# Second block's latent attention: the scores of the next two query tiles written ahead of the weighted sums, and the rotary parts of all heads projected first

## The chip, the cores and the metric

The kernel is one program on one core of a Trainium2 chip. The engines are TensorE (PE, with its weight loads shown apart as PEld), VectorE (DVE), ScalarE (ACT), GpSimd (POOL) and SyncE (SP), whose queue issues every DMA of the part that is changed. Each engine runs its instructions in the order in which the program holds them. The metric is the device time of one execution in microseconds (us); smaller is better.

## The reference, cut to what matters

Two blocks of two layers each on 512 tokens of width 1024. The change is in the latent attention ("MLA") of the second block, which runs once in each of its two layers: 4 heads, each query and key made of 128 plain and 64 rotary columns, and the rotary part of the key shared by all heads.

```
def mla_branch(c_q, c_kv, k_rope, pos, q_norm, w_uq, kv_norm, w_ukv):
    q = (rmsnorm(c_q, q_norm) @ w_uq).reshape(B, S, MLA_HEADS, MLA_NOPE + MLA_ROPE)
    q_nope = q[..., :MLA_NOPE]
    q_rope = apply_rope_2(q[..., MLA_NOPE:], pos)
    kv = (rmsnorm(c_kv, kv_norm) @ w_ukv).reshape(B, S, MLA_HEADS, MLA_NOPE + MLA_V)
    k_nope, v = kv[..., :MLA_NOPE], kv[..., MLA_NOPE:]
    k_r = apply_rope_2(k_rope, pos)
...
        s = (jnp.einsum('bqhd,bkhd->bhqk', qn, k_nope)
             + jnp.einsum('bqhr,bkr->bhqk', qr, k_r))
        prob = jax.nn.softmax(s.astype(jnp.float32) * scale, axis=-1).astype(v.dtype)
        return jnp.einsum('bhqk,bkhd->bqhd', prob, v)
```

The result is multiplied by a gate, joined with a gated linear attention ("GLA"), projected by `w_out`, and then a second gate multiplies a projection of a further input `p` ("PLE").

## The kernel before, in words

Every value is held as a pair of a rounded part and its rest, so that a product is three matmuls (high times high, high times low, low times high). `split` (L298 to L300) makes such a pair: ACT casts to the high part (L299), DVE subtracts it to get the low part (L300). `wload` (L170 to L188) loads weights by DMA into one of three raw buffers (`wr`), casts them on ACT (L183) and subtracts on DVE (L186).

The program is written in one order and then put in another: a scheduler takes the instructions with the priorities that the code gives, estimates when each can start, and writes each engine's order. It may move an instruction ahead of others that stand before it in the code, so what the code writes is not what the engines run.

`layer2` runs one layer. Generators for the two halves of the GLA, the output gates, the low-rank inputs, the key's rotation, the normalisation scales and the attention are advanced one step at a time by the string `steps2` (L93): `0` and `1` are GLA halves, `g` gates, `c` low-rank inputs, `r` `key_rope`, `l` `scales`, `m` and `v` steps of `mla`.

`rope2` (L1223) rotates a tile: it needs the tile with its 32-row groups swapped, which DMAs from SBUF to SBUF make (L1235 to L1238), then DVE multiplies by cosine and sine (L1241, L1242), adds (L1243), and splits. `scales` sums squares into one PSUM bank (`pv`), and `lowrank_scale` (L1207 to L1221) turns them into factors by small matmuls, five short DVE instructions (L1214 to L1220) and a power on POOL (L211). The factors of the keys are spread over a tile, `rkb` (L1117), by which every key is multiplied when it leaves PSUM (L1548).

In `mla`, `proj_head(h)` projects keys and queries of head h; for heads 0 and 2 it also projects and rotates the rotary parts of two heads. A head's 512 queries are taken as two units of two 128-row query tiles. For a unit the code writes the scores of each tile (six matmuls into a bank of tag `ps`) with its `softmax` (L495 and L497 on DVE, the exponential L499 on ACT, L501 on DVE, the scaling L502 on ACT), then the transposes of the four key blocks (L1614, into the banks `pt`, `ga`, `gb` in turn), their split, and the weighted sum (twelve matmuls into `pv`), which DVE multiplies into the gate (L1626). At a head's end the gated result is split (`C<-L`). The PLE projections (L1063) are written in the last head.

PSUM has eight banks: two for `pp` (all projections), two for `ps`, one each for `pt`, `pv`, `ga` and `gb`. A tile's bank is free for the next tile of its tag when its last reader is done. SBUF tiles of 512 columns come from rings: `M` (25 buffers), `C` (20), `L` (13).

Of the kernel before, what the change touches and what calls it, by code (L numbers as in the profile page):

```python
# [11 lines left out]
F32R = mybir.dt.float32r  # L12
# [3 lines left out]
ALU = mybir.AluOpType  # L16
# [4 lines left out]
P = 128  # L21
D = 1024
KT = 8
SEQ = 512
# [53 lines left out]
class Net:  # L78
# [11 lines left out]
             "kkkkqqccggthhccqqiiccppppppggthhccqqiikkkkccppppppggthhccqqiiccppppppggthhcciipppppp")  # L90


    steps2 = "00" + "g0g1g" + "01g0" + "0100" + "cccc" + "1rlm" + "g1g1g1g1" + "v1"  # L93
    bprio, sprio = 300, 500
    wshare_mla = 0

# [31 lines left out]
    def al(self, role, dt=F32):  # L128
        pool, tag, bufs, w = self.roles[role]
        return pool.tile([P, w], dt, tag=tag, bufs=bufs, name=self.nm(tag))  # L130
# [912 lines left out]
        return xs  # L1043


    def ple_proj(self, l):

        nc = self.nc
        xs = []
        for k in range(2):  # L1050
            x = self.C()
            nc.sync.dma_start(x, self.a["pT"][l, k])
            h = (self.C(F32R), self.C(F32R))
            self.split(h[0], h[1], x)
            xs.append(h)
        out = []
        for c in range(2):
            w = self.wload(self.a["w_ple_proj"][l, c], 2, 512)
            for i in range(4):
                ps = self.ps("pp")  # L1060
                self.proj(ps, w, i * P, (i + 1) * P, xs, [(0, SEQ)])
                y = self.C()
                nc.scalar.activation(y, ps, AF.Copy, scale=0.5)  # L1063
                out.append(y)
        return out

    def trig(self):

# [151 lines left out]
        nc.vector.tensor_tensor(z, y, r, ALU.mult)  # L1220
        return z  # L1221

    def rope2(self, src, n, al, tmp):  # L1223


        nc = self.nc
        if n == P:
            x = tmp()
            nc.scalar.copy(x, src)
            rot, own = x, src  # L1230
        else:
            rot, own = src, tmp()
            for b in range(0, P, n):
                nc.sync.dma_start(own[b:b + n, :], src[0:n, :])
        sw = tmp()  # L1235
        for b in range(0, P, 32):
            o = (b ^ 32) % n
            nc.sync.dma_start(sw[b:b + 32, :], rot[o:o + 32, :])  # L1238
        y = tmp()
        for i, c in enumerate((slice(0, 256), slice(256, 512))):  # L1240
            nc.vector.tensor_tensor(y[:, c], own[:, c], self.cos[i], ALU.mult)  # L1241
            nc.vector.tensor_tensor(sw[:, c], sw[:, c], self.sin[i], ALU.mult)  # L1242
        nc.vector.tensor_tensor(y, y, sw, ALU.add)  # L1243
        a, b = al(F32R), al(F32R)
        self.split(a, b, y)
        return a, b

    def layer2(self, l, h, st):
        nc, tc, a = self.nc, self.tc, self.a
        S4 = [(0, SEQ)]  # L1250
# [65 lines left out]
        kr = []  # L1316

        def key_rope():
            kr.append(self.rope2(sm, 64, self.M, self.C))
            yield  # L1320

        ms, sc = [None] * KT, {}
# [11 lines left out]
        pts = []  # L1334
# [191 lines left out]
    def mla(self, l, cq, ckv, kr, sc, sgd, md, ms, pts):  # L1526


        nc, a = self.nc, self.a
        S4 = [(0, SEQ)]  # L1530
        rkb, rkv, qsc = sc["kvb"], sc["kv"], sc["q"]
        krh, krl = kr[0]
        qr, qk = {}, {}
        wk = {}

        def proj_head(h):
            if h % 2 == 0:
                w = self.wload(a["w_uq"][l, 2], 3, 256)
                ps = self.ps("pp")
                self.proj(ps, w, (h // 2) * P, (h // 2 + 1) * P, cq, S4)  # L1540
                qr[h // 2] = self.rope2(ps, P, self.M, self.M)
                wk["q"] = self.wload(a["w_uq"][l, h // 2], 3, 256)
                wk["k"] = self.wload(a["w_ukv"][l, 0][:, :, 256 * (h // 2):256 * (h // 2) + 256], 2, 256)
            m = slice((h % 2) * P, (h % 2 + 1) * P)
# [10 lines left out]
            qk[h] = (kh, kl, qh, ql)  # L1555

        proj_head(0)
        yield

        w = self.wload(a["w_ukv"][l, 1], 2, 512)  # L1560
        vs = []
        for t in range(4):
            ps = self.ps("pp")
            for k in range(2):
                xh, xl = ckv[k]
                c = slice(t * P, (t + 1) * P)
                self.mm(ps, xh[:, c], w.hi(k, 0, 512), k == 0, False)
                self.mm(ps, xh[:, c], w.lo(k, 0, 512), False, False)
                self.mm(ps, xl[:, c], w.hi(k, 0, 512), False, k == 1)
# [4 lines left out]
            vs.append((vh, vl))  # L1574
        yield
        for h in range(4):
            if h < 3:
                proj_head(h + 1)
            else:
                pts += self.ple_proj(l)  # L1580
            if h == 2:
                for hd in range(4, 8):
                    t = self.C()
                    nc.sync.dma_start(t, md[hd])
                    x, y = self.L(F32R), self.L(F32R)
                    self.split(x, y, t)
                    ms[hd] = (x, y)
            kh, kl, qh, ql = qk.pop(h)
            rh, rl = qr[h // 2]
            rr = slice(64 * (h % 2), 64 * (h % 2) + 64)  # L1590
            sg = self.L()
            nc.sync.dma_start(sg, sgd[h])
            for tp in range(2):
                pr = []
                for j in range(2):
                    t = 2 * tp + j
                    c = slice(t * P, (t + 1) * P)
                    ps = self.ps("ps")
                    self.mm(ps, qh[:, c], kh, True, False)
                    self.mm(ps, qh[:, c], kl, False, False)  # L1600
                    self.mm(ps, ql[:, c], kh, False, False)
                    self.mm(ps, rh[rr, c], krh[rr], False, False)
                    self.mm(ps, rh[rr, c], krl[rr], False, False)
                    self.mm(ps, rl[rr, c], krh[rr], False, True)
                    p = self.M()
                    self.softmax(ps, SEQ, qsc[:, t:t + 1], p)
                    pr.append(p)
                po = self.ps("pv")
                for kk in range(0, 4, 2):
                    self.npt += 1  # L1610
                    pt = self.ps(("pt", "ga", "gb")[self.npt % 3])
                    for i in range(2):
                        for j in range(2):
                            nc.tensor.transpose(pt[:, i * 256 + j * P:i * 256 + (j + 1) * P],  # L1614
                                                pr[j][:, (kk + i) * P:(kk + i + 1) * P], self.ident)
                    ph, pl = self.M(F32R), self.M(F32R)
                    self.split(ph, pl, pt)
                    for i in range(2):
                        kt = kk + i
                        vc = slice(h * P, (h + 1) * P)  # L1620
                        ss = slice(i * 256, (i + 1) * 256)
                        self.mm(po[:, :256], vs[kt][0][:, vc], ph[:, ss], kt == 0, False)
                        self.mm(po[:, :256], vs[kt][0][:, vc], pl[:, ss], False, False)
                        self.mm(po[:, :256], vs[kt][1][:, vc], ph[:, ss], False, kt == 3)
                sc = sg[:, tp * 256:(tp + 1) * 256]
                nc.vector.tensor_tensor(sc, po[:, :256], sc, ALU.mult)  # L1626
            al = self.C if h < 3 else self.L
            x, y = al(F32R), al(F32R)
            self.split(x, y, sg)
            ms[h] = (x, y)  # L1630
            yield


# [125 lines left out]
```

## Time and profile before

| what | value |
|---|---|
| median of 3 runs | 3402.8 us (3402.74 to 3403.55) |
| the profiled execution, its own time | 3398.06 us |
| span of the profiled execution | 3396.3 us |
| mean granted TensorE clock | 0.962 of full speed |
| TensorE matmul busy | 3189.1 us (94%) |
| VectorE busy | 2134.7 us (63%) |
| ScalarE busy | 1414.4 us (42%) |

The span is what the hardware profiler saw between the first and the last instruction; the execution's own time lies 1.8 us above it, and 4.7 us below the median of the runs. A busy share is an average over stages with different limits. The granted clock is 1.0 at 2.4 GHz and 0.5 at 1.2 GHz, TensorE's two levels; a number between them is a mean over a stretch.

### The profile page before, as it was taken

How to read it: one execution, taken by the hardware profiler on the slowest of the kernel's cores; microseconds unless marked ns; L12 is line 12 of the kernel's file. 1: busy time of each engine (PE TensorE's matmuls, PEld its weight loads, DVE VectorE, ACT ScalarE, POOL GpSimd, SP SyncE). 2: the span in 40 equal slices, each digit the busy share in tenths (PEclk: the TensorE clock that was granted, in tenths of full speed). 3: DMA queues.
4: the chain of work that ended last, by engine and by line, in shares of the span. 5: the costliest groups of instructions: out<-in, count | busy, mean ns of one | idle time of the engine just before them, and what ended most of it. 6: DMA issues, size and time to landing. Idle time of an engine off the chain costs nothing. (4 is left out here: it accounts for less than half of the span.)

```text
span 3396.3 us, 46629 instructions
## 1 busy us (share of the span) xinstructions
PE 3189.1 (94%) x18622; PEld 2663.2 (78%) x18622; DVE 2134.7 (63%) x3158; ACT 1414.4 (42%) x2406; POOL 413.2 (12%) x489
## 2 busy tenths in 40 slices
PE   7999999999999999998999989899998898998898
PEld 4887887878778888887888867888887666996677
DVE  6795968744554444446997966755556655666555
ACT  3444343444432122224444445532346435564464
POOL 2130322201000000002112311000001200122001
PEclk8999998999999999998999999999998998999999
DMA  6232312133333432232222233433243232442323
GB/s 254 70 125 84 122 58 69 60 118 101 100 118 132 141 119 63 60 109 88 72 70 91 78 121 113 150 98 99 88 126 110 88 99 70 156 155 80 99 91 119
DMA packets 112808, 353.45 MB, mean 104 GB/s; under 512 B 13328, under 2 KB 20048, under 8 KB 107472
## 3 DMA queue, kind: packets, MB, share of 16 engines
q1 hardware_dynamic: 112592, 350.48, 32.1%
q8 instruction: 146, 2.39, 0.3%
q14 instruction: 70, 0.57, 0.1%
HBM read 327.10 MB, written 21.23 MB: 103 GB/s over the span
## 5 line engine op out<-in xcount | busy, mean ns | idle before, releaser
L186 DVE TENSOR_TENSOR wl<-wr,wh 128x1024 fp32r<-128x1024 f32 (+1 forms) x482 | 582.7, 1211 | 354.8 <-ACT wh L183 350.2
L183 ACT CAST wh<-wr 128x1024 fp32r<-128x1024 f32 (+1 forms) x482 | 490.8, 1020 | 739.3 <-PE pp L191 692.7
L191 PE MATMUL pp<-A,wh 128*128 128x512 f32 (+1 forms) x3392 | 779.8, 345 | 14.5 <-DVE A L296 5.2
L191 PE MATMUL pp<-C,wh 128*128 128x512 f32 (+1 forms) x2328 | 650.6, 366 | 27.5 <-DVE M L1548 11.0
L191 PEld LDWEIGHTS pp<-A,wh 128*128 128x128 f32 x3392 | 537.1, 190 | 127.3 <-issue 19.7
L191 PEld LDWEIGHTS pp<-C,wh 128*128 128x128 f32 x2328 | 414.8, 192 | 111.3 <-DVE M L1548 12.7
L191 PE MATMUL pp<-A,wl 128*128 128x512 f32 (+1 forms) x1696 | 463.2, 342 | 0.0
L191 PE MATMUL pp<-C,wl 128*128 128x512 f32 (+1 forms) x1164 | 421.3, 363 | 0.0
L191 PE MATMUL pp<-B,wh 128*128 128x512 f32 (+1 forms) x1296 | 316.7, 351 | 0.1
L191 PE MATMUL pp<-M,wh 128*128 128x256 f32 (+1 forms) x1280 | 294.3, 325 | 14.5 <-ACT M L1132 7.1
L191 PEld LDWEIGHTS pp<-A,wl 128*128 128x128 f32 x1696 | 272.6, 190 | 41.5 <-issue 1.9
L599 DVE SCALAR_TENSOR_TENSOR W<-W,cw,W 128x783 f32<-128x783 f32 x240 | 275.5, 1152 | 2.6
L191 PEld LDWEIGHTS pp<-C,wl 128*128 128x128 f32 x1164 | 222.3, 191 | 36.6 <-issue 1.1
L191 PEld LDWEIGHTS pp<-M,wh 128*128 128x128 f32 x1280 | 217.2, 196 | 42.4 <-issue 10.4
L191 PEld LDWEIGHTS pp<-B,wh 128*128 128x128 f32 x1296 | 212.3, 188 | 38.4 <-issue 2.1
L211 POOL TENSOR_TENSOR s<-s,nhalf 128x2 f32<-128x2 f32 (+4 forms) x40 | 54.4, 1360 | 1433.7 <-DVE s L277 1416.4
L191 PE MATMUL pp<-M,wl 128*128 128x256 f32 (+1 forms) x640 | 204.8, 321 | 0.0
L599 DVE SCALAR_TENSOR_TENSOR W<-U,cw,W 128x512 f32<-128x512 f32 x240 | 192.8, 804 | 3.5
L191 PE MATMUL pp<-B,wl 128*128 128x512 f32 (+1 forms) x648 | 194.0, 351 | 0.0
L886 DVE SCALAR_TENSOR_TENSOR B<-pp,cols,B 128x511 f32<-128x511 f32 x66 | 43.4, 658 | 214.7 <-ACT B L883 214.7
L851 DVE SCALAR_TENSOR_TENSOR X<-pp,g,X 128x512 f32<-128x512 f32 (+1 forms) x128 | 77.0, 631 | 146.9 <-PE pp L191 146.6
L883 ACT ACTIVATE B<-pp,cols 128x768 f32<-128x768 f32 (+1 forms) x44 | 38.9, 885 | 231.0 <-PE pp L191 231.0
(402 smaller groups left out, 4753.8 us busy)
## 6 DMA issues: line engine op xcount, KB each, us to landing
wr<-w_in SPq DMA_DIRECT2D x184, 512.0 KB, 3.8
wr<-w_up SPq DMA_DIRECT2D x96, 512.0 KB, 3.8
wa<-w_ada SPq DMA_DIRECT2D x40, 1024.0 KB, 5.0
wr<-w_out SPq DMA_DIRECT2D x64, 512.0 KB, 3.9
wr<-w_down SPq DMA_DIRECT2D x48, 512.0 KB, 3.6
wr<-w_ple_gate SPq DMA_DIRECT2D x32, 512.0 KB, 3.9
Z<-w_ada SPq DMA_DIRECT2D x16, 512.0 KB, 8.4
wr<-conv_pw SPq DMA_DIRECT2D x16, 512.0 KB, 3.8
```

The lines of the kernel that those rows point to most:

```text
L183: nc.scalar.copy(hi[:, :n], raw[:, :n])
L186: eng.tensor_tensor(lo[:, :n], raw[:, :n], hi[:, :n].bitcast(F32), ALU.subtract)
L191: return self.nc.tensor.matmul(out, l, r, start=start, stop=stop)
L211: self.nc.gpsimd.tensor_tensor(y, x, self.nhalf[:, :n], ALU.pow)
L599: nc.vector.scalar_tensor_tensor(y, gl[:, i:i + no], ws[:, i:i + 1], y, ALU.mult, ALU.add)
L851: nc.vector.scalar_tensor_tensor(xs[t][:, c0:c0 + sn], ps[:, c0:c0 + sn], g5[:, t, q:q + 1], xs[t][:, c0:c0 + sn], ALU.mult, ALU.add)
L883: nc.scalar.activation(y[:, :n], pa[:, :n], AF.Identity, bias=self.col(l, "fdw_b")[:, f:f + 1], scale=cw[:, 1:2])
L886: nc.vector.scalar_tensor_tensor(y[:, c0 + 1:e], pa[:, c0:e - 1], cw[:, 0:1], y[:, c0 + 1:e], ALU.mult, ALU.add)
```

## The change

The code of one unit is cut in two functions, `scores(h, tp)` and `weighted(h, tp, pr, sg)`. The loop over the eight units of a layer writes the scores of the next unit before the weighted sum of the present one. `rope2` is cut into `rope_rows` (copy out of PSUM and the swapping DMAs) and `rope_turn` (the arithmetic, now in place and thus one tile less). `query_rows` projects the rotary parts of all four heads, from one load of their weights, before head 0; their `rope_turn` stands after the value projections. The key's rotation is a step ahead of `scales`, its arithmetic behind it (`1rlrm`). The PLE projections are written in two portions, one in each unit of the last head, and the loads of the four GLA results one at a time after units 3 to 6.

```
-    steps2 = "00" + "g0g1g" + "01g0" + "0100" + "cccc" + "1rlm" + "g1g1g1g1" + "v1"
+    steps2 = "00" + "g0g1g" + "01g0" + "0100" + "cccc" + "1rlrm" + "g1g1g1g1" + "v1"
...
-    def rope2(self, src, n, al, tmp):
+    def rope_rows(self, src, n, tmp):
+        nc = self.nc
+        own, sw = tmp(), tmp()
         if n == P:
-            x = tmp()
-            nc.scalar.copy(x, src)
-            rot, own = x, src
+            nc.scalar.copy(own, src)
+            rot = own
...
+        return own, sw
+
+    def rope_turn(self, own, sw, al):
...
+            nc.vector.tensor_tensor(own[:, c], own[:, c], self.cos[i], ALU.mult)
...
         def key_rope():
-            kr.append(self.rope2(sm, 64, self.M, self.C))
+            rows = self.rope_rows(sm, 64, self.C)
+            yield
+            kr.append(self.rope_turn(*rows, self.M))
             yield
...
+        def query_rows():
+            w = self.wload(a["w_uq"][l, 2], 3, 256)
+            rows = []
+            for i in range(2):
+                ps = self.ps("pp")
+                self.proj(ps, w, i * P, (i + 1) * P, cq, S4)
+                rows.append(self.rope_rows(ps, P, self.M))
+            return rows
         def proj_head(h):
             if h % 2 == 0:
-                w = self.wload(a["w_uq"][l, 2], 3, 256)
-                ps = self.ps("pp")
-                self.proj(ps, w, (h // 2) * P, (h // 2 + 1) * P, cq, S4)
-                qr[h // 2] = self.rope2(ps, P, self.M, self.M)
...
+        units = [(h, tp) for h in range(4) for tp in range(2)]
+        emb = self.ple_proj(l, pts)
+        pr = scores(*units[0])
+        for (h, tp), then in zip(units, units[1:] + [None]):
+            if tp == 0:
+                sg = self.L()
+                nc.sync.dma_start(sg, sgd[h])
+                if h < 3:
+                    proj_head(h + 1)
+            if h == 3:
+                next(emb)
+            if then is not None:
+                if then[1] == 0:
+                    del qk[h]
+                ahead = scores(*then)
+            weighted(h, tp, pr, sg)
+            pr = ahead
+            if 3 <= 2 * h + tp <= 6:
+                linear_head(2 * h + tp + 1)
+            if tp == 1:
+                al = self.C if h < 3 else self.L
+                x, y = al(F32R), al(F32R)
+                self.split(x, y, sg)
+                ms[h] = (x, y)
             yield
```

What the engines run is shown at three places of the first layer; the second layer stands alike there, and outside the attention stretches of the two layers the engines' orders are the same but for names and the place of one matmul. First, DVE where head 2 starts, after the second unit of head 0. `pp` are projections of head 2, `M_23868` its rotary tile before, `L` and `C` the gated result of head 0. Before:

```order
L1241 TENSOR_TENSOR M_23868<-pp_23851,X_18048 128x256
L1241 TENSOR_TENSOR M_23868<-pp_23851,X_18052 128x256
L1626 TENSOR_TENSOR L_23707<-pv_23809,L_23707 128x256
L300 TENSOR_TENSOR C_23842<-L_23707,C_23841 128x512
L1242 TENSOR_TENSOR M_23863<-M_23863,X_18056 128x256
L1242 TENSOR_TENSOR M_23863<-M_23863,X_18060 128x256
L1243 TENSOR_TENSOR M_23868<-M_23868,M_23863 128x512
L300 TENSOR_TENSOR M_23875<-M_23868,M_23874 128x512
L1548 TENSOR_TENSOR M_23897<-pp_23890,rkb_23287 128x512
```

Of the change, the same head's keys leaving PSUM, now at L1557:

```order
L1608 TENSOR_TENSOR L_23738<-pv_23801,L_23738 128x256
L300 TENSOR_TENSOR M_23874<-pt_23868,M_23873 128x512
L495 TENSOR_REDUCE s_23952<-ps_23944 128x1
L300 TENSOR_TENSOR M_23889<-ga_23883,M_23888 128x512
L1557 TENSOR_TENSOR M_23924<-pp_23917,rkb_23277 128x512
L497 TENSOR_TENSOR s_23954<-s_23952,s_23261 128x1
L300 TENSOR_TENSOR M_23927<-M_23924,M_23926 128x512
L300 TENSOR_TENSOR M_23941<-pp_23930,M_23940 128x512
L1608 TENSOR_TENSOR L_23738<-pv_23867,L_23738 128x256
```

The key evacuation no longer stands behind the five instructions of a rotation; those are now before the first unit.

Second, PE inside a unit. `ps` is a score tile of a later unit, `pt`, `ga` and `gb` are transposes of probabilities, and `pv` sums. Before:

```order
L191 MATMUL ps_23936<-M_23251,M_23324 128x512
L1614 MATMUL pt_23810<-ident,M_23799 128x128
L1614 MATMUL pt_23810<-ident,M_23782 128x128
...
L1614 MATMUL ga_23825<-ident,M_23799 128x128
L1614 MATMUL ga_23825<-ident,M_23782 128x128
...
L191 MATMUL pv_23809<-M_23815,G_23613 128x256
L191 MATMUL pv_23809<-M_23816,G_23613 128x256
```

Of the change:

```order
L191 MATMUL ps_23961<-M_23289,M_23658 128x512
L191 MATMUL pv_23867<-M_23873,G_23619 128x256
L1596 MATMUL gb_23979<-ident,M_23857 128x128
L1596 MATMUL gb_23979<-ident,M_23840 128x128
...
L191 MATMUL pv_23867<-M_23874,G_23619 128x256
L191 MATMUL pv_23867<-M_23873,G_23629 128x256
...
L1596 MATMUL pt_23994<-ident,M_23840 128x128
```

Before, a unit's sum followed its own transposes with nothing between them, and the scores of the next unit stood ahead of both. Now the sum is of the unit before the one that is transposed: it stands a whole unit behind its own transposes.

Third, ACT at the end of head 1. `C` is the high part of that head's gated result `L`, `M<-M` and `M<-pp` are keys and queries of head 3, and the `ACTIVATE` on `ps` is the exponential that frees a score bank. Before:

```order
L299 CAST M_24064<-M_24062 128x512
L299 CAST M_24078<-pp_24068 128x512
L299 CAST C_24051<-L_23917 128x512
L499 ACTIVATE M_24115,s_24120<-ps_24108,s_24118,s_23271 128x512
L502 ACTIVATE M_24115<-M_24115,s_24122 128x512
L499 ACTIVATE M_24132,s_24137<-ps_24125,s_24135,s_23271 128x512
```

Of the change:

```order
L299 CAST M_24097<-M_24095 128x512
L299 CAST M_24111<-pp_24101 128x512
L299 CAST C_24082<-L_23903 128x512
L499 ACTIVATE M_24122,s_24127<-ps_24115,s_24125,s_23261 128x512
L502 ACTIVATE M_24122<-M_24122,s_24129 128x512
L299 CAST L_24183<-C_24181 128x512
L499 ACTIVATE M_24139,s_24144<-ps_24132,s_24142,s_23261 128x512
```

Here the order is the same but for the cast of a GLA result (`L<-C`) that now stands between the two exponentials.

## Rows read from the trace of the kernel before

**Rows 1.** The page: span, and busy time by engine.

```profile
span 3396.3 us, 46629 instructions
PE 3189.1 (94%) x18622; PEld 2663.2 (78%) x18622; DVE 2134.7 (63%) x3158; ACT 1414.4 (42%) x2406; POOL 413.2 (12%) x489
```

**Rows 2.** Stretches (start:end length), busy us (instructions) by engine, granted clock, DMA.

```profile
2720.00:2745.00 25.00, 19.84 (x114) 14.84 (x115) 17.06 (x53) 5.37 (x15) 2.75 (x3) 0.90 0.17 52
2787.00:2866.00 79.00, 68.27 (x295) 47.13 (x294) 43.80 (x96) 46.52 (x87) 1.05 (x2) 0.87 0.18 61
3120.00:3147.00 27.00, 21.39 (x129) 16.05 (x128) 18.89 (x57) 6.09 (x14) 3.80 (x5) 0.92 0.32 101
3190.00:3270.00 80.00, 69.95 (x307) 48.63 (x306) 45.28 (x96) 47.74 (x89) 0.00 (x0) 0.87 0.18 61
```

**Rows 3.** PE's waits, 2716 to 2870: total us, times, longest.

```profile
PE pp L191 <- DVE M L1548: 5.8, 2, 4.7
PE pv L191 <- DVE s L1220: 2.7, 1, 2.7
PE ps L191 <- ACT M L499: 2.1, 1, 2.1
PE pv L191 <- ACT M L299: 1.7, 5, 0.3
PE pv L191 <- DVE M L300: 1.7, 5, 0.3
PE pp L191 <- DVE s L1214: 1.6, 1, 1.6
```

**Rows 4.** PE's waits in the second layer, 3118 to 3273.

```profile
PE pp L191 <- DVE M L1548: 5.2, 2, 4.0
PE ps L191 <- ACT M L499: 2.0, 1, 2.0
```

**Rows 5.** PE in order of time: start, us, instruction, [idle before <-releaser].

```profile
2810.25 1.22 PE L191 MATMUL pp<-C,wh 128*128 128x512 f32 x2 [4.70 <-DVE M L1548]
...
2815.11 0.46 PE L191 MATMUL pp<-C,wl 128*128 128x512 f32 x1
...
2816.11 1.75 PE L191 MATMUL ps<-M,M 128*128 128x512 f32 x6
...
2820.97 0.38 PE L191 MATMUL pv<-M,G 128*128 128x256 f32 x1 [0.35 <-ACT M L299]
2821.70 1.58 PE L191 MATMUL pv<-M,G 128*128 128x256 f32 x11 [0.34 <-DVE M L300]
2823.11 1.75 PE L191 MATMUL ps<-M,M 128*128 128x512 f32 x6
...
2832.32 3.22 PE L191 MATMUL ps<-M,M 128*128 128x512 f32 x6 [2.05 <-ACT M L499]
...
2843.76 2.73 PE L191 MATMUL ps<-M,M 128*128 128x512 f32 x6
```

**Rows 6.** DVE in order of time, head 2's start.

```profile
2806.74 0.76 DVE L1242 TENSOR_TENSOR M<-M,X 128x256 f32<-128x256 f32 x2 [1.45 <-DMA M<-M]
...
2811.49 0.68 DVE L300 TENSOR_TENSOR M<-pp,M 128x512 fp32r<-128x512 f32 x1
```

**Rows 7.** ACT in order of time, end of head 1.

```profile
2830.40 0.58 ACT L299 CAST M<-pp 128x512 fp32r<-128x512 f32 x1
2830.88 0.62 ACT L299 CAST C<-L 128x512 fp32r<-128x512 f32 x1
2831.40 0.78 ACT L499 ACTIVATE M<-ps,s,s 128x512 f32<-128x512 f32 x1
2832.07 0.20 ACT L499 ACTIVATION_READ_ACCUMULATOR M<-ps,s,s 128x1 f32 x1
2832.64 0.72 ACT L502 ACTIVATE M<-M,s 128x512 f32<-128x512 f32 x1 [0.37 <-DVE s L501]
```

**Rows 8.** PE in order of time, end of the scale chain.

```profile
2740.94 2.05 PE L191 MATMUL pv<-ident,s 128*128 128x128 f32 x8 [2.74 <-DVE s L1220]
```

More of the change, by code (lines that the diff above doesn't have):

```diff
@@ L1043, in block1, with ple_proj @@
         return xs
-    def ple_proj(self, l):
+    def ple_proj(self, l, out):
         nc = self.nc
@@ L1055, in ple_proj @@
             xs.append(h)
-        out = []
         for c in range(2):
@@ L1064, in ple_proj @@
                 out.append(y)
-        return out
+            yield
     def trig(self):
@@ L1221, in lowrank_scale @@
         return z
-    def rope2(self, src, n, al, tmp):
+    def rope_rows(self, src, n, tmp):
         nc = self.nc
+        own, sw = tmp(), tmp()
         if n == P:
-            x = tmp()
-            nc.scalar.copy(x, src)
-            rot, own = x, src
+            nc.scalar.copy(own, src)
+            rot = own
         else:
-            rot, own = src, tmp()
             for b in range(0, P, n):
                 nc.sync.dma_start(own[b:b + n, :], src[0:n, :])
-        sw = tmp()
+            rot = src
         for b in range(0, P, 32):
@@ L1238, in rope2 @@
             nc.sync.dma_start(sw[b:b + 32, :], rot[o:o + 32, :])
-        y = tmp()
+        return own, sw
+    def rope_turn(self, own, sw, al):
+        nc = self.nc
         for i, c in enumerate((slice(0, 256), slice(256, 512))):
-            nc.vector.tensor_tensor(y[:, c], own[:, c], self.cos[i], ALU.mult)
+            nc.vector.tensor_tensor(own[:, c], own[:, c], self.cos[i], ALU.mult)
             nc.vector.tensor_tensor(sw[:, c], sw[:, c], self.sin[i], ALU.mult)
-        nc.vector.tensor_tensor(y, y, sw, ALU.add)
+        nc.vector.tensor_tensor(own, own, sw, ALU.add)
         a, b = al(F32R), al(F32R)
-        self.split(a, b, y)
+        self.split(a, b, own)
         return a, b
@@ L1318, in key_rope @@
         def key_rope():
-            kr.append(self.rope2(sm, 64, self.M, self.C))
+            rows = self.rope_rows(sm, 64, self.C)
+            yield
+            kr.append(self.rope_turn(*rows, self.M))
             yield
@@ L1531, in mla @@
         rkb, rkv, qsc = sc["kvb"], sc["kv"], sc["q"]
-        krh, krl = kr[0]
         qr, qk = {}, {}
         wk = {}
+        def query_rows():
[6 more added lines that the diff above has]
+            return rows
         def proj_head(h):
             if h % 2 == 0:
-                w = self.wload(a["w_uq"][l, 2], 3, 256)
-                ps = self.ps("pp")
-                self.proj(ps, w, (h // 2) * P, (h // 2 + 1) * P, cq, S4)
-                qr[h // 2] = self.rope2(ps, P, self.M, self.M)
                 wk["q"] = self.wload(a["w_uq"][l, h // 2], 3, 256)
@@ L1555, in proj_head, with scores, weighted, linear_head @@
             qk[h] = (kh, kl, qh, ql)
+        def scores(h, tp):
+            kh, kl, qh, ql = qk[h]
+            rh, rl = qr[h // 2]
+            krh, krl = kr[0]
+            rr = slice(64 * (h % 2), 64 * (h % 2) + 64)
+            pr = []
+            for j in range(2):
+                t = 2 * tp + j
+                c = slice(t * P, (t + 1) * P)
+                ps = self.ps("ps")
+                self.mm(ps, qh[:, c], kh, True, False)
+                self.mm(ps, qh[:, c], kl, False, False)
+                self.mm(ps, ql[:, c], kh, False, False)
+                self.mm(ps, rh[rr, c], krh[rr], False, False)
+                self.mm(ps, rh[rr, c], krl[rr], False, False)
+                self.mm(ps, rl[rr, c], krh[rr], False, True)
+                p = self.M()
+                self.softmax(ps, SEQ, qsc[:, t:t + 1], p)
+                pr.append(p)
+            return pr
+        def weighted(h, tp, pr, sg):
+            po = self.ps("pv")
+            for kk in range(0, 4, 2):
+                self.npt += 1
+                pt = self.ps(("pt", "ga", "gb")[self.npt % 3])
+                for i in range(2):
+                    for j in range(2):
+                        nc.tensor.transpose(pt[:, i * 256 + j * P:i * 256 + (j + 1) * P],
+                                            pr[j][:, (kk + i) * P:(kk + i + 1) * P], self.ident)
+                ph, pl = self.M(F32R), self.M(F32R)
+                self.split(ph, pl, pt)
+                for i in range(2):
+                    kt = kk + i
+                    vc = slice(h * P, (h + 1) * P)
+                    ss = slice(i * 256, (i + 1) * 256)
+                    self.mm(po[:, :256], vs[kt][0][:, vc], ph[:, ss], kt == 0, False)
+                    self.mm(po[:, :256], vs[kt][0][:, vc], pl[:, ss], False, False)
+                    self.mm(po[:, :256], vs[kt][1][:, vc], ph[:, ss], False, kt == 3)
+            c = slice(tp * 256, (tp + 1) * 256)
+            nc.vector.tensor_tensor(sg[:, c], po[:, :256], sg[:, c], ALU.mult)
+        def linear_head(hd):
+            t = self.C()
+            nc.sync.dma_start(t, md[hd])
+            x, y = self.L(F32R), self.L(F32R)
+            self.split(x, y, t)
+            ms[hd] = (x, y)
+        rows = query_rows()
         proj_head(0)
@@ L1574, in mla @@
             vs.append((vh, vl))
+        for i in range(2):
+            qr[i] = self.rope_turn(*rows[i], self.M)
         yield
[L1576 to L1630, printed above, removed]
```

## The prediction, made before the change was run

> **What bounds the kernel now.** I read the page first: PE is busy 94% of the span, and no other engine is above 63% [rows 1]. So time can come only from PE: from its waits, from stretches in which its clock is low, or from work taken off it. The change takes no matmul away. I therefore went to the two stretches that it touches and read their granted clock, then PE's waits there, then the order of time around each wait.
>
> The attention of the first layer lies at 2787 to 2866. PE is busy 68.3 of its 79 us at a mean clock of 0.87, DVE 43.8 and ACT 46.5, so neither of these is full; the second layer has the same numbers [rows 2]. The scales and the first head's projections lie just before, at 2720 to 2745, with clock 0.90, and at 3120 to 3147 with 0.92 [rows 2]. The waits [rows 3] fall into four kinds.
>
> One: 4.70 us at 2805 to 2810, where PE waits for the keys of head 2 to leave PSUM (L1548). DVE stood still 1.45 us for the swapped rows of the query's rotation to land, and the key stood behind that rotation in its order [rows 5, 6]. With the smaller one for head 1 that is 5.8 us. Two: ten waits of some 0.34 us, two in each of five units, 3.4 us: the sum of a unit follows its own transposes, so PE waits for the cast and then for the subtraction [rows 3, 5]. Three: 2.05 us at the end of head 1. A score tile needs a bank that the exponential of an earlier tile frees, and that exponential stands on ACT behind the cast of the gated result, which waits for the sum that PE has just finished [rows 5, 7]. Four: 1.6 and 2.7 us in the scale chain [rows 3, 8].
>
> Then the clock. After the 4.70 us, matmuls run at the low level from 2810.25 until about 2815.1; after the 2.05 us, six score matmuls take 3.22 us where they took 1.75, and this lasts until 2846 [rows 5]. A unit at full clock takes 2823.11 - 2816.11 = 7.0 us, 0.69 of it waits; the one at 2832.32 takes 11.44. The same places are low in the second layer, by its clock.
>
> **The change part by part.**
>
> *Rotary parts first.* The nine matmuls for heads 2 and 3 move ahead of head 0: no change of PE's work. One weight load per layer with its cast and subtraction goes; ACT and DVE have over 30 us free in either attention stretch [rows 2], so it is worth nothing either way, from below because no wait of [rows 3] names a weight there. What the move buys is the wait of kind one: in the new DVE order the keys of head 2 leave PSUM behind plain splits and a reduction, all of which are ready; no DMA stands between. I take the whole 5.8 us, and 5.2 in the second layer [rows 4], whose other waits of these kinds are those of [rows 3], row for row. The swaps go out on SP behind the same loads as before; eight in a row instead of four, but they are needed only by the next unit's scores, some 30 us later. The cover is the output gates' projections, and without it the 1.45 us would come back.
>
> *Sums a unit later.* The sum's operands were transposed, cast and subtracted a whole score tile earlier, so kind two goes: 3.4 us per layer. What would bring it back is ACT or DVE falling a unit behind; a unit needs twice 0.78 + 0.20 + 0.72 for the softmax and twice 0.58 for casts on ACT, 4.6 us, against 6.3 us of PE (7.0 less 0.69), so there is room [rows 5, 7].
>
> *The score bank.* Kind three is not touched. At the end of head 1 ACT still has the two casts of head 3, then the cast of the gated result, then the exponential that frees the bank, and PE still goes straight from the sum to that score tile. I keep the 2.05. Behind it ACT now has one more cast, 0.6 us, ahead of the next exponential: another 0.6 us of PE wait, and some 0.25 us at the first units, where the exponential of unit 1 stands behind the projections of head 1. Together 0.85, between 0 and about 2 (one more cast and one exponential).
>
> *The end of the last head.* Before, PLE projections filled PE while the last softmax ran. Now they stand behind the last-but-one sum. The chain behind the first of the last two score tiles is exponential 0.98, scaling 0.72, exponential 0.98, cast 0.58, subtraction 0.68 = 3.9 us [rows 6, 7], behind a reduction on DVE that I put at 0.7 like the subtraction; PE has one score tile and a unit's transposes and sum, 1.75 + (6.3 - 3.5) = 4.5 us, to put over these 4.6. Counted so, 0.1 us shows. But the casts and subtractions of the unit before stand in front of that chain, 2 x 0.58 + 2 x 0.68 = 2.5 us, in the same two orders. Between 0.1 and 2.6 I take 2.6, since nothing else in PE's order lies between.
>
> *The scale chain.* The key scales' small matmuls now come earlier, but with two new neighbours: the second group waits for the first to leave the one `pv` bank, on DVE behind a weight subtraction, and the key's own evacuation stands behind two rotations of queries and two masked copies. What PE waits there lies between 0, if all is ready in time, and the 4.3 of before (1.6 + 2.7). I take three quarters, 3.3: DVE's order, POOL's power and the one bank, which made the chain before, are all still in it. It should come in three pieces (the bank of the sums, a bank of the GLA, the key's evacuation), none above 1.5.
>
> *The clock.* What low clock costs in a stretch is its length times the part missing: 79 x 0.13 = 10.3 us in the first layer's attention, 25 x 0.10 = 2.5 in the scale chain; 80 x 0.13 = 10.4 and 27 x 0.08 = 2.2 in the second [rows 2]. Of the 10.3, the stretch behind the 2.05 us wait has 11.44 - 6.31 = 5.1, and 2.73 - 1.75 = 1.0 for the next tile, 6.1 in all [rows 5]; as the wait stays, I let this stay. Behind the 4.70 us there is half of 4.9 us, 2.4, which goes. In the scale chain the drop came behind 1.6 and 2.7 us [rows 3, 8]; in the new order I expect no single wait above 1.5 there, and the 1.1 us for head 1 (5.8 - 4.7) left the clock full. So 2.4 + 2.5 = 4.9 us come back in the first layer, 2.4 + 2.2 = 4.6 in the second.
>
> **Sum.** First layer: 5.8 + 3.4 + 4.3 - 3.3 - 0.85 - 2.6 + 4.9 = 11.65. Second: 5.2 + 3.4 + 4.3 - 3.3 - 0.85 - 2.6 + 4.6 = 10.75. Together 22.4 us, against the profiled execution's own 3398.06, which gives 3375.7; the median of the runs lies 4.7 us higher at 3402.8, so the forecast is 3402.8 - 22.4 = 3380.4, say 3380.
>
> **Short waits and the clock.** The rows show full speed through units with two waits of 0.35 us each (1.75 us for the scores at 2816.11 and 2823.11), and a drop behind 2.05 us and more [rows 5]. By the Trainium skill, "TensorE: Matmul & The Clock Gate", section "A second HAM failure mode: psum-queue depth-cycling", it would be otherwise: small idle times between groups of matmuls that turn through PSUM banks make the clock go up and down. By that rule alone the change, which puts short waits at the last head and in the scale chain, would give back less; the trace does not bear it out for 0.35 us, and shows nothing for 1.0 to 1.5 us in a row. Without the page, the case stands below.
>
> **The rivals.**
> *The clock stays full behind the bank wait too.* The new order has no other idle time in the units before it. Then 6.1 us more per layer: 3380 - 12 = 3368. Against it: both layers fell at that place before.
> *The groups of short waits pull the clock down.* If the last head (its 2.6 us in several waits close together) and the scale chain both lose 2.4 us as behind the 4.70, that is 4 x 2.4 = 10 us: 3390.
> *It does not do what it says.* PE's order before already had the next unit's scores ahead of the sum: 2823.11 is a score tile of a later unit. If the new waits eat all that goes (each stretch keeps its waits in another form and the clock its lows), the time is 3398 to 3403. Against it: the rotation's DMA wait, with its clock the largest single thing, is gone from the order whatever else happens.
> *Slower: every head's end stalls on the score bank.* The mechanism is kind three, at the ends of heads 0 and 2 as well: 2.05 and 6.1 us of clock, 8.1 each. Two more per layer cost 32 us: 3380 + 32 = 3412. It decides from three such stalls over both layers, as 3 x 8.1 is more than 22.4. Against it: at the end of head 0, fifteen projection matmuls stand between the sum and the next score tile, and the exponential stands ahead of the cast; at head 2, no score tile follows.
>
> **How the numbers follow.** The forecast has 0.49, full clock 0.20, short waits 0.18, no effect 0.07, slower 0.06. About 0.2%, 6.8 us, is what a measurement of this kernel can tell from no change; the first three cases lie beyond that, so faster is 0.87, same 0.07, slower 0.06. The range takes in the first three: down to 3364 for the full clock with less than 2.6 us at the last head, and up to 3394 for the short waits with the bounds of the bank wait.
>
> **What would show it.** The wait of `pp` on the key evacuation at head 2 gone, and the rotation's arithmetic ahead of the first unit; the pairs of 0.34 us gone, a unit near 6.3 us; one wait of about 2 us on L499 left per layer at the end of head 1, with the clock low behind it; about 2.6 us of waits on L299 and L300 by the last two sums. The prediction is wrong if units take over 7 us with the clock full, if DVE waits for a rotation's DMA elsewhere, or if the clock falls at places that have only short waits.

## The result and the profile after

The changed kernel takes 3359.4 us (median, 3357.4 to 3363.8) against 3402.8 us before: ratio 0.9878, 95% interval 0.9866 to 0.9891, 43 us less. Timed twice more, on two chips, it came to 0.9886 (0.9866 to 0.9906) and 0.9886 (0.9871 to 0.9902), 37 and 39 us less. The forecast was 22.4 us and 3380, the range ended at 3364: the sign was right, the gain came out 1.9 times as large, and 1.6 and 1.7 times in the two repeats.

The page of the changed kernel, to be set against [rows 1]: the same matmuls, 20 us less of busy PE, and a span shorter by 40.7 us.

```profile
span 3355.6 us, 46619 instructions
...
PE 3168.9 (94%) x18622; PEld 2653.3 (79%) x18622; DVE 2128.9 (63%) x3156; ACT 1411.3 (42%) x2404; POOL 414.4 (12%) x489
```

To find where it came from I cut each layer at two fixed points of the program: from the last matmul pair `pv<-M,ones` of the scales to the first matmul of the output projection (`pp<-L,wh`). Between them lie the scale chain, the values and all heads. Length, then busy PE, with its matmuls, further on the clock; before, two layers:

```profile
2720.24:2871.74 151.50, 134.53 (x616) 99.13 (x617) 83.21 (x181) 71.45 (x142) 6.17 (x8) 0.91 0.24 76
3123.43:3274.43 151.00, 134.64 (x615) 98.97 (x616) 83.63 (x181) 71.56 (x142) 5.63 (x7) 0.91 0.25 81
```

After:

```profile
2718.75:2851.94 133.19, 127.32 (x616) 96.24 (x616) 81.56 (x180) 70.40 (x142) 6.29 (x8) 0.95 0.26 86
3103.68:3234.33 130.65, 124.38 (x617) 93.68 (x616) 81.35 (x180) 70.09 (x142) 5.08 (x5) 0.97 0.26 87
```

The two stretches give 18.3 + 20.35 = 38.7 of the 40.7 us. Length less busy time is PE's idle time: 17.0 and 16.4 us before, 5.9 and 6.3 after, so 21.2 us are waits that went. The same matmuls were busy for 7.2 and 10.3 us less: 17.5 us are the clock and, by what is left over, shorter busy time at the same clock. The forecast had 12.9 us of waits and 9.5 of clock.

PE's waits after, first layer's stretch (total us, times, longest), where [rows 3] had 17 us:

```profile
PE ps L191 <- ACT M L499: 3.3, 4, 1.9
PE ps L191 <- DVE L L1468: 1.1, 1, 1.1
PE pv L191 <- DVE s L501: 0.5, 1, 0.5
PE pp L191 <- DVE M L1557: 0.3, 1, 0.3
PE pp L191 <- ACT C L1062: 0.2, 1, 0.2
PE pv L191 <- DVE M L300: 0.2, 1, 0.2
```

The key evacuation (now L1557) has fallen from 5.8 us to 0.3, the pairs on L299 and L300 are gone, and the score bank (L499) is what is left. PE in order of time, first layer: start, us, instruction, idle before.

```profile
2725.80 1.14 PE L191 MATMUL ps<-C,M 128*128 128x256 f32 x2 [1.11 <-DVE L L1468]
...
2795.95 1.75 PE L191 MATMUL ps<-M,M 128*128 128x512 f32 x6
...
2801.78 0.62 PE L191 MATMUL pp<-C,wh 128*128 128x512 f32 x2
...
2819.01 1.85 PE L191 MATMUL ps<-M,M 128*128 128x512 f32 x6 [1.94 <-ACT M L499]
...
2821.50 3.22 PE L191 MATMUL ps<-M,M 128*128 128x512 f32 x6 [0.38 <-ACT M L499]
2824.65 1.65 PE L191 MATMUL pv<-M,G 128*128 128x256 f32 x6
...
2828.63 1.75 PE L191 MATMUL ps<-M,M 128*128 128x512 f32 x6
...
2835.20 0.36 PE L191 MATMUL pv<-M,G 128*128 128x256 f32 x1 [0.50 <-DVE s L501]
2835.77 0.87 PE L191 MATMUL pv<-M,G 128*128 128x256 f32 x5 [0.21 <-DVE M L300]
```

Here the reader sees the bank wait where the forecast put it, 1.94 us for 2.05 [rows 5]. Behind it six score matmuls take 3.22 us, the low level, but from 2828.63 on they take 1.75 again: low for about 7 us, where before it was 14. A unit takes 2801.78 - 2795.95 = 5.8 us (7.0 before, 6.3 forecast). ACT in order of time shows why the wait stayed:

```profile
2816.10 0.62 ACT L299 CAST M<-M 128x512 fp32r<-128x512 f32 x1 [1.35 <-DVE M L1557]
2816.62 0.58 ACT L299 CAST M<-pp 128x512 fp32r<-128x512 f32 x1
2817.57 0.62 ACT L299 CAST C<-L 128x512 fp32r<-128x512 f32 x1 [0.37 <-DVE L L1608]
2818.10 0.77 ACT L499 ACTIVATE M<-ps,s,s 128x512 f32<-128x512 f32 x1
```

The exponential that frees the bank stands behind the casts of head 3's keys and of the gated result of head 1, as in [rows 7].

### The profile page after: what moved, and what is told of

Its sections match the earlier page's. It is cut to its first block, busy times and chain, and to the rows that moved or that the text cites. A ratio compares the mean times of both kernels' runs of the same rounds, so it can differ in the third digit from the quotient of the medians.

```text
span 3355.6 us, 46619 instructions
## 1 busy us (share of the span) xinstructions
PE 3168.9 (94%) x18622; PEld 2653.3 (79%) x18622; DVE 2128.9 (63%) x3156; ACT 1411.3 (42%) x2404; POOL 414.4 (12%) x489
## 5 line engine op out<-in xcount | busy, mean ns | idle before, releaser
L851 DVE SCALAR_TENSOR_TENSOR X<-pp,g,X 128x512 f32<-128x512 f32 (+1 forms) x128 | 76.9, 631 | 146.9 <-PE pp L191 146.7
```

The source lines that it names most:

```text
L851: nc.vector.scalar_tensor_tensor(xs[t][:, c0:c0 + sn], ps[:, c0:c0 + sn], g5[:, t, q:q + 1], xs[t][:, c0:c0 + sn], ALU.mult, ALU.add)
```

## The experiments

All twelve in one table. "Idle" is PE's idle time in the stretch above, first and second layer. "Low" is the time at the low clock from the first score tile to the output projection: twice (1 - granted clock) times the length, over pieces of 5 us, summed, and rounded to whole us; before, 7 of it lie behind the keys' wait and 14 behind the bank wait. Half of it is lost when PE is busy in it. Runs of one letter shared a chip with the kernel before, which took 3400.3 (e), 3401.8 (f) and 3400.2 us (h) there.

| kernel | median us | ratio to before | idle | low | stretch |
|---|---|---|---|---|---|
| before | 3402.8 | | 17.0 / 16.4 | 20 / 21 | 151.5 / 151.0 |
| after | 3359.4 | 0.9878 | 5.9 / 6.3 | 7 / 0 | 133.2 / 130.7 |
| e1 rotary alone | 3386.9 | 0.9956 | 9.4 / 9.6 | 10 / 24 | 140.1 / 146.8 |
| e2 scores ahead alone | 3375.9 | 0.9932 | 10.3 / 11.5 | 10 / 3 | 138.7 / 137.5 |
| e3 after, casts on POOL | 3365.9 | 0.9899 | 7.0 / 6.0 | 10 / 7 | 132.1 / 134.3 |
| e4 after, keys a unit earlier | 3362.5 | 0.9891 | 4.9 / 4.8 | 7 / 0 | 132.4 / 129.9 |
| f1 after again | 3365.2 | 0.9886 | 5.9 / 5.4 | 7 / 10 | 133.2 / 134.0 |
| f2 before, three banks | 3399.5 | 0.9995 | 16.1 / 17.1 | 21 / 3 | 150.6 / 143.6 |
| f3 rotary, three banks | 3387.1 | 0.9946 | 9.6 / 11.6 | 14 / 10 | 141.5 / 143.0 |
| f4 keys earlier, three banks | 3359.2 | 0.9871 | 5.8 / 5.7 | 0 / 0 | 129.3 / 130.2 |
| h1 rotary, keys earlier | 3375.1 | 0.9930 | 9.6 / 9.1 | 0 / 10 | 137.0 / 140.5 |
| h2 rotary again | 3385.8 (one) | | 9.4 / 9.5 | 10 / 24 | 140.1 / 146.7 |
| h3 as f4, again | 3361.5 | 0.9886 | 5.8 / 5.7 | 7 / 0 | 132.4 / 130.2 |
| h4 after, third time | 3361.0 | 0.9886 | 5.9 / 5.4 | 7 / 10 | 133.2 / 134.0 |

**The two parts apart.** e1 keeps the rotary part and goes back to one unit after the other; the PLE projections stand ahead of the last head and the GLA loads ahead of head 2 again, as before:

```diff
-        pr = scores(*units[0])
-        for (h, tp), then in zip(units, units[1:] + [None]):
...
+        for h in range(4):
...
+            for tp in range(2):
+                weighted(h, tp, scores(h, tp), sg)
```

> The rotary part of the change alone: queries of all heads projected and rotated ahead of the first head, but every unit's scores, softmax and sum in a row as before, and all PLE projections ahead of the last head's first scores as before. By the prediction's own terms this part is nearly the whole change: waits 5.8 and 5.2, 1.0 a layer in the scale chain, clock 4.9 and 4.6, together 22.5 us, so 3380, and the sums a unit later would be worth about nothing. Theory A (the excess of 21 us came from the sums a unit later, above all because the low clock behind the score-bank wait ends early when the units behind it hold no waits): 3380 here too, the pairs of 0.34 us back, the clock low for about 13 us behind the 2 us wait in both layers. Theory B (the 4.7 us wait of the keys of head 2, gone here, is what made the later low clock long): 3365 to 3370, and the low clock behind the 2 us wait lasts 7 us or less.

e2 keeps the units, with the PLE projections in two portions, and puts back each pair's rotary projection, swap and rotation; the key's rotation is in one piece again:

```diff
         def proj_head(h):
             if h % 2 == 0:
+                query_rows(h // 2)
...
-        rows = query_rows()
```

> The scores given a unit ahead alone, with the PLE projections in the last head's units: the rotary part stays as before, projected and rotated for two heads at a time inside the projections of heads 0 and 2, and the key's rotation has one piece as before. By the prediction's terms this part is worth 3.4 - 0.85 - 2.6 a layer, nothing: 3403. Theory A: about 21 us, 3382, and low clock behind the bank wait 7 us or less, but a wait of 4 to 5 us on the key's evacuation at head 2 with low clock of some 5 us behind it. Theory B: under 12 us, 3391 to 3400, with the long low clock behind the bank wait back in both layers.

The stretches of e1 and e2 (columns as above):

```profile
2721.35:2861.44 140.09, 130.74 (x616) 96.54 (x616) 81.99 (x180) 71.47 (x142) 6.29 (x8) 0.94 0.24 81
3116.41:3263.21 146.80, 137.19 (x623) 100.84 (x622) 82.37 (x181) 71.82 (x142) 5.97 (x7) 0.90 0.25 82
```

```profile
2722.83:2861.48 138.65, 128.38 (x616) 96.21 (x616) 82.47 (x181) 70.73 (x142) 5.95 (x8) 0.95 0.25 83
3118.01:3255.48 137.47, 125.94 (x615) 94.03 (x616) 82.41 (x181) 70.43 (x142) 5.42 (x7) 0.96 0.27 88
```

The rotary part alone is worth 11.4 + 4.2 = 15.6 us of these stretches (15 us by its ratio), the scores ahead alone 12.85 + 13.5 = 26.4 (23 by its ratio). Together 42.0, near the 38.7 of both. By the prediction's terms they were 22.5 and nothing. Of the 15.6, 14.4 are waits (forecast 13.0); only 1.2 us are busy time, where 9.5 of clock were to come back (its second stretch holds eight small matmuls more). Of the 26.4, 14.9 are busy time. The 7 us of low clock behind the keys' wait went with that wait in e1, in both layers, but behind the bank wait 14 and 14 us became 10 and 24, so that little came back in all. The granted clock of whole executions says the same: 262 us at the low level before (35 executions, mean clock 0.9615), 264 in e1 and h2 (seven, 0.9610). Theory B falls: e1 has no 4.70 us wait and is low for 24 us behind its bank wait in the second layer:

```profile
3220.20 2.77 PE L191 MATMUL ps<-M,M 128*128 128x512 f32 x6 [2.04 <-ACT M L499]
```

e2 still has a keys' wait; in order of time, with its bank wait split in two:

```profile
2810.60 0.73 PE L191 MATMUL pp<-C,wh 128*128 128x512 f32 x2 [3.10 <-DVE M L1554]
...
2828.74 1.39 PE L191 MATMUL ps<-M,M 128*128 128x512 f32 x4 [0.65 <-DVE M L300]
...
2830.97 2.62 PE L191 MATMUL ps<-M,M 128*128 128x512 f32 x6 [0.58 <-ACT M L499]
```

Theory A had the right part for most of the gain, but its mechanism falls too. It said that waits in the units keep the clock low. In e1's 24 us PE is busy nearly throughout, and the clock stays down all the same; stretches of 5 us with busy times and clock:

```profile
3219.89:3224.89 5.00, 4.69 (x12) 2.56 (x12) 3.69 (x10) 4.53 (x10) 0.00 (x0) 0.59 0.00 0
3224.89:3229.89 5.00, 4.82 (x15) 3.38 (x16) 2.86 (x6) 2.29 (x5) 0.00 (x0) 0.50 0.02 3
3229.89:3234.89 5.00, 5.00 (x17) 3.50 (x16) 1.46 (x5) 1.97 (x4) 0.00 (x0) 0.50 0.00 0
3234.89:3239.89 5.00, 4.89 (x13) 2.70 (x12) 0.93 (x4) 1.24 (x3) 0.00 (x0) 0.50 0.00 0
3239.89:3244.89 5.00, 4.93 (x17) 3.96 (x17) 2.75 (x8) 2.91 (x7) 0.00 (x0) 0.52 0.00 0
```

**The bank wait shortened.** e3 moves two casts away from ACT:

```diff
-            self.split(kh, kl, kn)
+            self.split(kh, kl, kn, nc.gpsimd.tensor_copy if h == 3 else None)
...
-                self.split(x, y, sg)
+                self.split(x, y, sg, nc.gpsimd.tensor_copy if h == 1 else None)
```

> The changed kernel, with two casts per layer moved from ACT to POOL: the cast of head 1's gated result and that of head 3's keys, which stood ahead of the exponential that frees the score bank. If those two casts make the bank wait, it falls from 1.94 us to about 1.1 (then the subtraction of head 3's keys on DVE ends last). Theory A: waits 0.8 less a layer, and the low clock behind it (2.9 us in the first layer) gone if the shorter wait leaves it full: 3354 to 3358. If the bank wait's length does not set the clock: 3358, low clock as in the changed kernel. Slower than 3364 if POOL's cast takes so long that the keys come later than before.

e4 projects a unit earlier (head 1 behind the first scores):

```diff
-                if h < 3:
-                    proj_head(h + 1)
+            if tp == 1 and h < 2:
+                proj_head(h + 2)
```

> The changed kernel, with each next head's key and query projections one unit earlier (head 1's behind the first scores, head h+2's in the second unit of head h). The casts of head 3's keys then lie a unit before the exponential that frees the score bank, and only the cast of the gated result is left ahead of it. Theory A: the bank waits (2.3 us a layer with the 0.38) halve or go, and with them the 2.9 us of low clock in the first layer: 3350 to 3355. If what is waited for is the sum itself (the gated cast behind it), the wait stays near 1.9 us: 3357 to 3362. If the rings of 25 tiles hold the keys up instead: new waits on PE, 3365 or more.

In e3 the wait on L499 fell from 3.3 to 1.5 us (longest 0.8), with 0.8 on the subtraction of the keys, as expected; so those casts did make it. But a wait of 2.3 us appeared at the last head of the first layer, the clock was low in both layers, and 3354 to 3358 did not come: other orders moved too, and nothing was won. In e4 the bank waits are 2.1 us (longest 0.8) for 3.3. Behind the two at the end of head 1 the clock fell in the first layer, as it did behind 1.94, and stayed full in the second (last two lines):

```profile
2813.36 1.87 PE L191 MATMUL ps<-M,M 128*128 128x512 f32 x6 [0.55 <-ACT M L499]
...
2816.28 3.22 PE L191 MATMUL ps<-M,M 128*128 128x512 f32 x6 [0.60 <-ACT M L499]
...
2823.30 1.75 PE L191 MATMUL ps<-M,M 128*128 128x512 f32 x6
...
3201.25 1.85 PE L191 MATMUL ps<-M,M 128*128 128x512 f32 x6 [0.56 <-ACT M L499]
...
3204.16 1.86 PE L191 MATMUL ps<-M,M 128*128 128x512 f32 x6 [0.60 <-ACT M L499]
```

Its stretches are 0.8 us shorter each, by their waits; the whole time is that of the changed kernel within its interval, and not the 3350 to 3355 of theory A.

**The bank wait and the old order.** f1 is the changed kernel again. f2 and f3 give the kernel before and e1 a third score bank:

```diff
-                ps = self.ps("ps")
+                self.nsc += 1
+                ps = self.ps(("ps", "ps", "gb")[self.nsc % 3])
...
-                pt = self.ps(("pt", "ga", "gb")[self.npt % 3])
+                pt = self.ps(("pt", "ga")[self.npt % 2])
```

f4 is e4 with the same edit.

> The changed kernel as it is, once more, on the chip of the three runs below, to see how much of its gain is the clock's chance. If the low stretches belong to places of the program, the granted clock is low for about 7 us behind the bank wait of the first layer and not at all in the second, as in its first profile, and the time is 3357 to 3364. If they are chance, one of them comes out 0 or over 10 us, and the time moves by half of the difference.

> The kernel before, with score tiles turning over three banks of PSUM (the transposes then over two): its bank wait of 2 us at the end of head 1 should go, all else stays in order. If that wait makes the long low clock there (13.7 us in the first layer, 14 in the second), both go: 2.0 and some 6.9 us a layer, 17.9 in all, 3382 to 3385. If the low clock has another cause (the scores, transposes and one-piece sums of the units themselves), only the wait goes: 3396 to 3400. If transposes over two banks wait instead, 3402 or more.

> The rotary part alone, with score tiles over three banks as in the run above: sums still stand in one piece behind their own transposes. If the bank wait cost the rotary part its clock (low for 10 us in the first layer and 22 in the second), 2.8 us of waits and 5 and 11 us of clock come back: 3387 - 21.6 = 3365, within 6 us of the whole change. If the units' own order keeps the clock low, 3381 or more.

> The changed kernel with the keys a unit earlier and score tiles over three banks: no score tile should wait for an exponential. Against the run with the keys earlier alone (3362.5), 2.1 us of waits a layer and the 3.5 us of low clock in the first layer go: 3353 to 3356, faster than the changed kernel. If transposes over two banks wait for casts instead: 3360 or more.

f2 and f3 missed their aim: the wait of 2.0 us is still there, since the tile still needs an exponential that stands behind the same casts. So they settle nothing about a kernel without it, and 3382 and 3365 did not come. But the second layer of f2 shows something else. Same order, same wait, and the clock does not fall:

```profile
3238.30 1.87 PE L191 MATMUL ps<-M,M 128*128 128x512 f32 x6 [2.04 <-ACT M L499]
...
3240.33 1.84 PE L191 MATMUL ps<-M,M 128*128 128x512 f32 x6
```

Its first layer, with a 2.0 us wait at the same place, was low for 14 us. f1 shows the same in the changed kernel: the second layer, full in the first profile, is now low for 10 us, and its stretch 3.3 us longer. f4 has the full clock at the heads in both layers, as expected, and stretches of 129.3 and 130.2 us; its median, 3359.2, lies above the 3353 to 3356 expected, with bank waits of 1.4 us left in each layer and one of 2.0 us on L299 at the last head of the first.

**The last four.** h1 gives e1 the earlier keys, by the edit of e4 (head h + 2 ahead of the second unit); h2 to h4 repeat e1, f4 and the changed kernel.

> The rotary part alone, with each next head's projections half a head earlier, so that only the cast of the gated result is left ahead of the exponential that frees the score bank. Chance theory (a wait of about 2 us at the end of head 1 is followed by low clock of any length from 0 to 22 us, longer on the average where each sum stands in one piece behind its own transposes): the bank wait falls from 2.0 to about 1 us or less as in the run with the keys earlier, and if that leaves the clock full, 2 us of waits and some 5 us of clock a layer come back: 3373. If the units' own pairs of 0.34 us bring the low clock anyway: 3381 to 3386, with low stretches of 10 us or more among the units.

> The rotary part alone, once more, for its low stretches alone: chance theory: other lengths than the 10 and 22 us of its first profile behind the same 2 us waits. If the length belongs to the place: 10 and 22 us again. Its waits should be the same to 0.1 us.

> The keys a unit earlier and three score banks on the changed kernel, once more, beside the changed kernel on the same chip. If no wait over 0.7 us at the end of head 1 leaves the clock full there, both attention stretches have it full again, and the time is 4 to 8 us below the changed kernel's. If the full clock was chance: within 2 us of it, with a low stretch in one of the layers.

> The changed kernel a third time. Its waits are the same to 0.1 us; low stretches behind the bank wait of 0 to 10 us in either layer, and of about 7 us in the scale chain of both, where the wait is 1.1 us; 3357 to 3366.

h1 has e1's idle time within 0.5 us in either layer and 24 us less of low clock; its two stretches are 9.3 us shorter, its median 12 us (9 by the ratios). Half of 24 us would be 12: so much does low clock cost at about the same idle time (the second stretch also lacks the small matmuls of e1's). Its bank wait is 1.5 us in both layers, and the clock fell in one of them:

```profile
2815.63 1.85 PE L191 MATMUL ps<-M,M 128*128 128x512 f32 x6 [1.52 <-ACT M L499]
...
3204.23 2.10 PE L191 MATMUL ps<-M,M 128*128 128x512 f32 x6 [1.53 <-ACT M L499]
...
3206.59 3.20 PE L191 MATMUL ps<-M,M 128*128 128x512 f32 x6
```

h2 contradicts the chance theory: e1's 10 and 24 us came back, its stretches to within 0.1 us. The lengths belong mostly to a kernel and a layer, and change now and then (the second layer of after: 0, 10, 10). h3 fell low in the first layer again, so f4's full clock was not secured, and against the changed kernel on the same chips (3359.2 to 3365.2, 3361.5 to 3361.0) it is no proven gain.

## Why the prediction was wrong, step by step

The 18.3 us between 40.7 and 22.4, by the prediction's terms, both layers, first profile of after:

| term | forecast | measured | missed |
|---|---|---|---|
| keys behind the rotation's DMA | 11.0 gone | gone | 0 |
| pairs of 0.34 us | 6.8 gone | gone | 0 |
| scale chain: left as waits | 6.6 | 2.7 (L1468, L1557) | 3.9 |
| score bank | 5.8 (2.05 + 0.85 a layer) | 6.6 | -0.8 |
| last head | 5.2 | 2.0 | 3.2 |
| other waits of before that went (L1204 0.7 a layer, some of 0.2 to 0.4), by difference | 0 gone | 2.0 gone | 2.0 |
| clock behind the 4.70 us | 4.8 back | back | 0 |
| clock of the scale chain | 4.7 back | none | -4.7 |
| clock behind the bank wait | 0 back | (13.7 - 6.8)/2 + 13.7/2 = 10.3 | 10.3 |
| busy time that the clock rows leave over | 0 | 17.5 - 15.1 | 2.4 |
| outside the two stretches | 0 | 40.7 - 38.7 | 2.0 |

The waits missed 8.3 us of it, the clock 5.6, the rest 4.4. In the profiles f1 and h4 the waits missed more, 9.2 us (11.2 us idle in both layers, for 12.1 here), and the clock next to nothing: 5.1 us came back behind the bank wait and none in the scale chain, where the prediction had it the other way round, so 9.9 us in all for 9.5. That this sum came out there is luck, two errors of 5 us against each other. The granted clocks of whole executions agree: 12 of the changed kernel have a mean of 0.9653, 233 us at the low level for 262 before. Half the difference, 14 us, is an estimate of the clock's share in a mean gain of 39; 25 us are left for waits and busy time, where the forecast had 12.9.

**Right.** The rotation's DMA wait and the pairs went as worked out, and e1 and e2 show it one by one: e1 loses the former and keeps the latter (1.7 + 1.7 us in its first layer), e2 the reverse, with 3.1 us a layer left of the former. The bank wait stayed, at the place and for the cause named.

**The steps that failed** are two. The one with the largest single term, in the first profile, is "as the wait stays, I let this stay": the 6.1 us of clock a layer behind the bank wait. It tied a length of low clock to the wait ahead of it. The runs show the wait at 2 us with 0 to 24 us of low clock behind it. What they show instead is that the length is no fixed part of the wait, and that it was shorter, on the average, in the new order. Where sums stand in one piece behind their own transposes and the wait is 2.0 us (before, e1, h2, f2, f3: ten places), the low clock behind it has a mean of 13 us. In the three profiles of after (six places, 1.9 us) it has 7: 7, 0, 7, 10, 7, 10. Half the difference is 3 us a layer. The first profile with 7 and 0 us got 10.3 back in all, the other two 5.1, a difference of the size of that between a gain of 43 us and of 37 or 39. With the scores ahead and bank waits under 1.1 us (e2, e3, e4, f4, h3: ten places) the mean is 3 us. But h1, in the old order with 1.5 us, has 0 and 10: the length goes with the wait too, the ranges overlap, and e1 and h2, like f1 and h4, are one kernel twice. That the order is what shortens it is not shown. Why the clock comes back sooner is not settled: idle time of PE within the low stretch does not explain it (e1's 24 us hold hardly any), and no run changed the order with every wait held.

**The same mistake the other way** is the scale chain, "no single wait above 1.5 there", so 2.5 and 2.2 us of clock were to come back. The waits shrank to 1.11 us, and the clock was low for 7 us as before, in both layers of each profile of the changed kernel. The prediction had named that, a fall where there are only short waits, as a sign of being wrong.

**The other step: terms mis-sized.** This one failed in every profile. Where the trace gave two bounds, I took the upper one for the last head (2.6 between 0.1 and 2.6; it measured 0.7 and 1.3) and three quarters of the old scale chain (3.3; 1.4 and 1.3). At the last head the price put the casts of the unit before in front of the last softmax; in the trace ACT had done them and stood idle for 2.47 us before that softmax's first exponential:

```profile
2828.29 0.57 ACT L299 CAST M<-pt 128x512 fp32r<-128x512 f32 x1
2831.34 0.78 ACT L499 ACTIVATE M<-ps,s,s 128x512 f32<-128x512 f32 x1 [2.47 <-DVE s L497]
```

For the scale chain no run shows why it waits so little. Other waits of before, 2.0 us, and the shorter busy time were not in the sum at all. Together with the clock that made the scores ahead worth nothing on paper; e2 shows that they, with the PLE portions, are the larger half.

**The rivals.** Of "the clock stays full behind the bank wait too" a part happened, but its 3368 would still have been 9 us too slow, by the waits. "Short waits pull the clock down" came true in the scale chain and not at the last head of the changed kernel. The Trainium skill, "TensorE: Matmul & The Clock Gate", section "A second HAM failure mode: psum-queue depth-cycling", says that small idle times between groups of matmuls that turn through PSUM banks make the clock swing. The first layer of e4 agrees (0.55 and 0.60 us on score banks, then 7 us low); its second (0.56 and 0.60, full clock) and the pairs of 0.34 us, at full clock in before and in e1, do not. No score bank stalled at the ends of heads 0 and 2 in a way that decided (L499 in all 3.3 us, longest 1.9).

## What to carry to other kernels

Where PE is the bound, cost a wait and the low clock behind it as two terms, and give the second a range from nothing to what the trace shows, since it can end sooner, or not come, with the wait still there. Read it in several profiles, and in the granted clock of every execution: one profile's low stretch may be another's full clock. And price the two halves of a change apart, with a build of each: a term that nets to nothing from three bounded guesses is the first to measure.

## What the runs showed of the hardware

With PE busy 4.7 to 5.0 us of every 5, the clock stayed at the low level (1.2 GHz) for 24 us in e1 and again in h2, at the same place. Behind a 2.04 us wait it did not fall at all in f2's second layer. In the scale chain of the new order a wait of 1.11 us, with eight matmuls of one column (0.95 us) shortly before it, came ahead of 7 us at the low level, in both layers of every profile of after. Executions of e1 spread from 3377 to 3392 us, more than most of the effects above.
